# Reading the banks of an attention kernel's filling units behind the next transposes' cast and low part

## The chip, the cores and the metric

One core of a Trainium2 chip runs the whole layer in one launch. The metric is the device time of one execution in microseconds, the median over several runs. A further execution was taken with the hardware profiler; its page and its trace are the source of all shares, waits and rows shown here. The core has a matrix engine (PE, with its weight loads shown as PEld), a vector engine (DVE), a scalar engine (ACT), a general engine (POOL), and SP, whose queue issues the transfers. PE writes to eight banks of PSUM, from which only ACT and DVE read.

## The reference

A decoder layer on 1024 tokens of width 1024: a half feed-forward block, then two kinds of attention side by side, gated and merged, then a second half feed-forward block and a gated embedding. The change lies in the attention stage:

```python
def forgetting_attention(q, k, v, log_f):          # 8 heads of 64; q and k are normalised first
    F = jnp.cumsum(log_f, axis=1)
    logits = q @ k.T * scale + F[t] - F[s]          # causal
    return softmax(logits) @ v

def stick_breaking_attention(q, k, v):             # 8 heads of 64
    z = q @ k.T * scale
    after = reverse_cumsum(log_sigmoid(-z)) - log_sigmoid(-z)
    return exp(log_sigmoid(z) + after) @ v          # strictly causal

merged = (sigmoid(g_fox) * (y_fox @ w_branch_fox)
          + sigmoid(g_sb) * (y_sb @ w_branch_sb))
```

All in float32. The kernel keeps that precision by splitting an operand into a high part, rounded to the matrix engine's float32r format, and a low part, the difference; a product is then three matmuls (high by high, high by low, low by high) or a stacked form of these.

## The kernel before

**Stages.** The first feed-forward block and the norm take about the first 660 us of the profiled execution, the attention loop the time from about 714 to 1376 us, and the branch products, the output product, the second block and the embedding the rest. The feed-forward blocks are written under a manual schedule, where program order is engine order. The attention loop is not: a planner, which has its own estimate of every duration, puts an instruction on its engine's queue when its inputs are ready by that estimate, and takes the one that comes first in program order where several are ready. `order(key, ins)` adds an edge from the last instruction given under the same key, so that instructions under one key ("pe", "act", "dve", "wh", "wl") stand on their queue in program order. All matmuls are under "pe". The queues themselves run in order.

**The loop.** Sixteen heads follow each other, 0 to 7 forgetting ("fox") and 8 to 15 stick-breaking. A head has four steps c = 0 to 3 of two blocks of 128 queries. `scores(step, ...)` makes the two blocks' score products into `sc` banks (L990, L991) and the weights from them: in fox heads a fused add and minimum on DVE (L995), the exponential on ACT (L1001) and a division on POOL (L1003); in stick-breaking heads two sigmoids on ACT (L998, L999), scans on DVE (L966) and products on POOL (L1013, L1017). `apply(prev, ...)` then finishes the step before: for each pair of key blocks, from the last pair down to 0, `transposes(kpair)` puts transposed weights into a `pt` bank (L1042), ACT casts them into a PT buffer (L1044, `high`), DVE subtracts for the low part (L1045, `low`), and `values(kpair + 1)` multiplies the pair before with the values into the `av` bank (L1058). At the end of a step three instructions gather the result from `av` (L1077 to L1079). The values product with both parts in one matmul, and the two additions at L1078 and L1079, stand in the kernel before and after alike.

In stick-breaking heads `high` is under "act" and `low` and the scans under "dve"; the scans of the odd block are held in `later`, and the first part of them is issued behind the first transposes of `apply` (`later.pop(0)()`), the rest behind the last. In fox heads `high` and `low` are under no key.

**Filling units.** Between these pieces PE would wait, so it gets other work: the projections for later heads. A unit is a generator that takes a `pf` bank (there are two), issues 24 matmuls (12 for a branch unit) one at a time, and then reads its bank. Kinds: values (`v_units`, L755, read by L112 and L113), queries and keys of a fox pair, with or without values (`fox_qk_units`, L755, read by L112, L113 and L844 to L846, and after each fourth unit L849 to L852 on DVE and POOL), stacks of a stick-breaking head in two halves (`sb_stack_units`, L763, read in `fill_stacks` by L862 to L865, with the copies L871 and L872 issued on SP), and gates (`g_units`, L763, read by L914 or, from gate 8 on, L916 into a PT buffer, stored by L917 on SP). Weights for the units come by L126 on SP and are split by L136 on ACT and L146 on POOL. PT has three buffers, shared by `high`/`low`, the gates and the squares of the fox units.

`take()` runs the units: the cost of a head's units (0.216 a matmul of 512 columns, 0.109 a smaller one) is divided by 22, and each call issues matmuls until its share is used up. In every head the calls are, for c = 0: one behind each of the two scores, one behind each of four transposes, one ahead of values(0); then 2 + 1 + 1 for c = 1, 2 + 2 + 1 for c = 2, 2 + 3 + 1 for c = 3: 22 in all. At the listed places of `TURNS` the stacks of the next fox head are also made (`fox_stack_units`, L882, which reads its bank on the spot by L867 to L870).

A head's units, as examples: head 8 has the two halves of stick-breaking head 9's stacks and three gate halves; head 10 three value units, two halves of stacks, two gate halves; head 14 one half of stacks, two gate halves, the other half of stacks, a gate half.

Of the kernel before, what the change touches and what calls it, by code (L numbers as in the profile page):

```python
# [11 lines left out]
F32R = mybir.dt.float32r  # L12
# [26 lines left out]
def tile_hybrid_decoder_layer(  # L39
# [56 lines left out]
    def f(ap):  # L96
        return ap.bitcast(F32)
# [667 lines left out]
                yield 0.216  # L765

    loads = []

    def add_load(cell, fn):
        cell["i"] = len(loads)  # L770
# [35 lines left out]
    def v_units(col, extra, cell):  # L806
        n = 256 + extra
        add_load(cell, lambda: mix_nat([(col, col + n)], NAT))

        def unit(t):  # L810
            weights(cell)
            if t == 0:
                cell["v"] = slot("X", [P, NT, 4, P], F32R)
            ps = bank("pf")
            yield from nat_steps(ps, t, cell["w"], n, hT)
            v_out(cell, t, ps[:, :256])
            if extra:
                nc.vector.tensor_copy(lfs[:, t, :], ps[:, 256:264])  # L818
        return [(24 * 0.109, unit(t)) for t in range(NT)]

    def fox_cols(pair):
# [2 lines left out]
    def fox_qk_units(pair, cell, col=None, vcell=None, sq_tag="PT"):  # L824
        cols = fox_cols(pair) + (((col, col + 256),) if col else ())
        nk = 2 if col else 4
        tags = (("WH", "WL"), ("WH", "WL"), ("WH", "WL"), ("Y", "RAW"))
        w = [stage([kp(win)[:, nk * i:nk * i + nk, a:b] for a, b in cols], nk, 1024 // nk, tags[i]) for i in range(KD // nk)]

        def unit(t):  # L830
            if t == 0:
                cell["n"] = [slot("RN", [P, 4, 2, 2, HD]) for _ in range(2)]
                cell["ss"] = [stat([P, 4, 4], "qkss", 4) for _ in range(2)]
            ps = bank("pf")
            yield from nat_steps(ps, t, cell["w"] if "w" in cell else [c["w"] for c in w], 1024 // nk, hT)
            if vcell is not None:
                if t == 0:
                    vcell["v"] = slot("X", [P, NT, 4, P], F32R)
                v_out(vcell, t, ps[:, 256:])
            half, q = divmod(t, 4)  # L840
            N = cell["n"][half]
            src = ps[:, :256].rearrange("p (s h d) -> p s h d", s=2, h=2)
            sq = slot(sq_tag, [P, 256])
            nc.scalar.activation(sq[:].rearrange("p (h s d) -> p s h d", s=2, h=2), src, AF.Square)  # L844
            nc.scalar.copy(N[:, q].rearrange("p h s d -> p s h d"), src)
            nc.vector.reduce_sum(cell["ss"][half][:, q, :], sq[:].rearrange("p (g d) -> p g d", g=4), axis=AX.X)  # L846
            if q == 3:
                ss = cell["ss"][half][:].rearrange("p a b -> p (a b)")
                nc.vector.tensor_scalar(ss, ss, 1.0 / HD, EPS, ALU.mult, ALU.add)  # L849
                nc.gpsimd.tensor_tensor(ss, ss, mhalf[:], ALU.pow)  # L850
                nv = N[:].rearrange("p a h s d -> p (a h s) d")
                nc.gpsimd.tensor_mul(nv, nv, ss.unsqueeze(2).broadcast_to([P, 16, HD]))  # L852
        return [(24 * (0.216 if col else 0.109), unit(t)) for t in range(NT)], w

    def new_stacks():
# [2 lines left out]
    def fill_stacks(stacks, ps, cs, gain=None):  # L858
        Q, KH, KL = stacks
        a, b = slice(0, HD), slice(HD, P)  # L860
        if gain is None:
            nc.scalar.copy(Q[a, cs], ps[a, :])  # L862
            nc.scalar.copy(KH[b, cs], ps[b, :])
            nc.vector.tensor_sub(Q[b, cs], ps[a, :], f(Q[a, cs]))
            nc.vector.tensor_sub(KL[b, cs], ps[b, :], f(KH[b, cs]))  # L865
        else:
            nc.scalar.activation(Q[a, cs], ps[a, :], AF.Copy, scale=gain[a, :])  # L867
            nc.scalar.activation(KH[b, cs], ps[b, :], AF.Copy, scale=gain[b, :])
            nc.vector.scalar_tensor_tensor(Q[b, cs], ps[a, :], gain[a, :], f(Q[a, cs]), ALU.mult, ALU.subtract)
            nc.vector.scalar_tensor_tensor(KL[b, cs], ps[b, :], gain[b, :], f(KH[b, cs]), ALU.mult, ALU.subtract)  # L870
        nc.sync.dma_start(f(KH[a, cs]), f(KH[b, cs]))  # L871
        nc.sync.dma_start(f(KL[a, cs]), f(KL[b, cs]))  # L872
# [14 lines left out]
    def sb_stack_units(head, out_cell):  # L887
        c0 = head * HD

        add_load(out_cell, lambda: wload([kp(win)[:, :, SQ + c0:SQ + c0 + HD], kp(win)[:, :, SK + c0:SK + c0 + HD]], KD, P))  # L890

        def unit(half):
            weights(out_cell)
            if half == 0:
                out_cell["st"] = new_stacks()
            ps = bank("pf")
            yield from feat_steps(ps, half, out_cell["w"])
            fill_stacks(out_cell["st"], ps, slice(half * 512, half * 512 + 512))
        return [(24 * 0.216, unit(0)), (24 * 0.216, unit(1))]

    def g_units(m, tags=None):
        cell = {}
        src = [kp(win)[:, :, GFOX + m * P:GFOX + m * P + P]]
        if tags:
            cell = stage(src, KD, P, tags)
        else:
            add_load(cell, lambda: wload(src, KD, P))

        def unit(half):
            ps = bank("pf")  # L910
            yield from feat_steps(ps, half, cell["w"] if tags else weights(cell))
            g = slot("PT", [P, 512])
            if m < KD:
                nc.vector.tensor_copy(g[:], ps[:])  # L914
            else:
                order("act", nc.scalar.activation(g[:], ps[:], AF.Sigmoid))  # L916
            nc.sync.dma_start(gd[m, :, half * 512:half * 512 + 512], g[:])  # L917
        units = [(24 * 0.216, unit(0)), (24 * 0.216, unit(1))]
        return (units, cell) if tags else units

# [106 lines left out]
    def apply(step, fill, later=()):  # L1027
# [32 lines left out]
        def turn_and_scan(kpair):  # L1060
            transposes(kpair)
            if later and kpair == c:
                later.pop(0)()
            fill()

        turn_and_scan(c)
# [62 lines left out]
    def attention():  # L1129
# [93 lines left out]
        load_fb(0)  # L1223
        ys = {}
        prev = None
        for h in range(16):
            fox = h < 8
            if h % 2 == 0:
                idx = fox_pairs[h // 2] if fox else 4 + (h - 8) // 2
                ys[h // 2] = {"t": slot("Y", [P, S]), "idx": idx}  # L1230
            head = ys[h // 2]["idx"] % 4 * 2 + h % 2
            v = (vf1, vf0, vs0, vs1)[h // 4]
            load_fb(h + 1)
            total = sum(u[0] for u in fill[h])
            state = [0.0 if h else 1.0, 0.0]
            gens = [u[1] for u in fill[h]]

            def take(last=False):
                state[0] += total / 22
                while gens and (last or state[1] < state[0]):  # L1240
                    cost = next(gens[0], None)
                    if cost is None:
                        gens.pop(0)
                    else:
                        state[1] += cost
            for c in range(4):
                y0, y1 = Y_AT.get((h, c), ((), ()))
                split_y(*y0)
                load_y(*y1)
                step = {"fox": fox, "c": c, "head": head, "st": stacks[h], "v": v, "y": ys[h // 2], "last": h == 15}  # L1250
                if fox:
                    step["fb"] = fbs[h]
                later = []
                calls = [0]

                def take_and_turn():
                    take()
                    if (h, c, calls[0]) in TURNS:
                        x, half = TURNS[h, c, calls[0]]
                        run(fst(x, "sc" if calls[0] else "av")[half][1])  # L1260
                    calls[0] += 1
                scores(step, take_and_turn, later if prev is not None else None)
                if prev is not None:
                    apply(prev, take_and_turn, later)
                if (h, c) == (4, 0):
                    place(c2w[3])
                prev = step
            take(True)
        rest = seq(*[g for _, g in fox_branch[8:]])
        apply(prev, lambda: run(islice(rest, 10)))  # L1270
        run(rest)
# [38 lines left out]
    def fox_branch_units():  # L1310
# [4 lines left out]
        def unit(m, half):  # L1315
            if half == 0:
                A.append(slot(("Q", "KH", "KL", "Y", "GF", "RN")[m], [P, S]))
            a = A[m]
            ps = bank("pf")
            yield from branch_steps(ps, 0, m, half, weights(cells[m]))  # L1320
            gated(a[:, half * 512:half * 512 + 512], ps, 0, m, half)
# [398 lines left out]
```

## Time and profile before

| | |
|---|---|
| median of 3 runs | 2234.88 us (2234.82 to 2235.48) |
| profiled execution | 2237.77 us |
| its span, first to last instruction | 2236.1 us |
| PE busy | 2215.4 us (99%) |
| DVE, ACT, POOL busy | 1512.9, 972.0, 812.8 us |
| mean granted TensorE clock | 0.999 |
| attention loop, PE busy in 732 to 1020 us (fox heads) | 277.99 of 288.00 us |
| the same in 1020 to 1376 us (stick-breaking heads) | 353.74 of 356.00 us |

How to read the rows: a line of the timeline has the start in us from the span's start, the duration in us, the engine, the kernel's line (L1045 is line 1045), the operation, output<-inputs, the shape and the count of instructions merged into the line, and in brackets the idle time of the engine just before, with what ended it. PE's ends are modelled and overlap the next start. A line of the waits has the waiting instruction, the one waited for, the total in us, how often, and the longest. A line of the stage table has the stretch, its length, and then the busy time of PE, PEld, DVE, ACT and POOL with their instruction counts, the granted clock, the transfer share and GB/s. "SPq" is SP issuing a transfer.

### The profile page before, as it was taken

The page shows a single profiled execution, that of the slowest core. Times are in us where ns is not written, and L with a number is a line of the kernel's source. Part 1 is how long each engine was busy: PE and PEld are TensorE (multiplying, and loading weights), DVE is VectorE, ACT ScalarE, POOL GpSimd, SP SyncE. Part 2 cuts the span into 40 slices and gives each one's busy share as a digit, 9 for nine tenths or more (in the row PEclk, how much of TensorE's full clock was granted, in tenths as well). Part 3 has the DMA queues.
Part 4 walks back from the last instruction along what each step waited for, and adds up shares of the span by engine and source line. Part 5 has one row for each costly group of instructions (what it writes and reads, how often), then busy time and mean ns, then how long its engine had stood idle before and what let it go on. Part 6 is the DMA issues. An engine that isn't in the chain of part 4 may idle for free.

```text
span 2236.1 us, 28590 instructions
## 1 busy us (share of the span) xinstructions
PE 2215.4 (99%) x10537; PEld 1842.1 (82%) x10537; DVE 1512.9 (68%) x2252; ACT 972.0 (43%) x1694; POOL 812.8 (36%) x709
## 2 busy tenths in 40 slices
PE   9999999999999999999999999999999999999999
PEld 7888888888889888877988888887888888888887
DVE  7855555497885665667667676899755555778873
ACT  6433333333453555455555564255333333433441
POOL 0344444310015456455556654400544443200111
PEclk9999999999999999999999999999999999999999
DMA  8232322484433023132124236741423232655132
GB/s 321 96 121 84 113 99 101 149 296 147 147 126 99 26 86 85 38 104 67 43 71 118 62 122 208 259 144 64 141 88 125 85 127 80 250 202 206 63 117 91
DMA packets 187709, 278.00 MB, mean 124 GB/s; under 512 B 27944, under 2 KB 110120, under 8 KB 187568
## 3 DMA queue, kind: packets, MB, share of 16 engines
q1 hardware_dynamic: 187568, 276.17, 36.8%
q8 instruction: 83, 1.36, 0.3%
q14 instruction: 58, 0.48, 0.1%
HBM read 192.47 MB, written 75.27 MB: 120 GB/s over the span
## 4 chain that ended last, share of the span: by engine, by line
PE 86%; DVE 6%; ACT 3%; issue 2%; DMA 1%; POOL 1%; SPq 0%; ACTq 0%; DVEq 0%; POOLq 0%
PE ps L496 36%; PE ps L388 19%; PE ps L763 8%; PE ps L755 6%; PE ps L1656 4%; PE ps L1301 3%; PE ps L1058 3%; PE ps L1042 2%; PE ps L449 2%; PE ps L991 1%; PE ps L990 1%; PE ps L1351 1%; DVE H L113 1%; DVE RN L966 1%; ACT H L112 1%
## 5 line engine op out<-in xcount | busy, mean ns | idle before, releaser
L388 PE MATMUL ps<-H,H 128*128 128x512 f32 x2184 | 497.3, 389 | 0.0
L388 PEld LDWEIGHTS ps<-H,H 128*128 128x128 f32 x2184 | 409.5, 188 | 84.9
L496 PE MATMUL ps<-H,WL 128*128 128x512 f32 x1008 | 238.9, 389 | 0.0
L496 PEld LDWEIGHTS ps<-H,WL 128*128 128x128 f32 x1008 | 189.2, 188 | 39.3
L763 PE MATMUL ps<-H,WH 128*128 128x512 f32 x640 | 175.9, 401 | 0.0
L1045 DVE TENSOR_TENSOR PT<-ps,PT 128x512 fp32r<-128x512 f32 (+1 forms) x160 | 100.8, 634 | 72.0 <-ACT PT L1044 71.0
L496 PE MATMUL ps<-H,Q 128*128 128x512 f32 x576 | 137.4, 389 | 0.0
L396 DVE SCALAR_TENSOR_TENSOR X<-ps,X 128x512 f32<-128x512 f32 x168 | 108.7, 685 | 41.8 <-PE ps L388 41.7
L763 PEld LDWEIGHTS ps<-H,WH 128*128 128x128 f32 x640 | 113.9, 188 | 19.1
L496 PEld LDWEIGHTS ps<-H,Q 128*128 128x128 f32 x576 | 108.1, 188 | 22.4
L1044 ACT CAST PT<-ps 128x512 fp32r<-128x512 f32 (+1 forms) x160 | 87.0, 548 | 87.3 <-PE ps L1042 82.2
L146 POOL TENSOR_TENSOR WL<-RAW,WH 128x512 fp32r<-128x512 f32 (+1 forms) x92 | 108.9, 1204 | 40.1 <-ACT WH L136 34.6
L496 PE MATMUL ps<-X,WL 128*128 128x512 f32 x480 | 115.5, 389 | 0.0
L209 POOL TENSOR_TENSOR PT<-PT,RN 128x1024 f32<-128x1024 f32 x2 | 4.8, 2402 | 295.1 <-ACT RN L203 295.1
L755 PE MATMUL ps<-WH,H 128*128 128x256 f32 (+2 forms) x576 | 111.2, 323 | 0.2 <-DVE log_f L818 0.2
L1003 POOL TENSOR_TENSOR T<-T,l 128x128 f32<-128x128 f32 (+3 forms) x64 | 73.3, 1147 | 100.1 <-DVE l L1002 99.2
L496 PEld LDWEIGHTS ps<-X,WL 128*128 128x128 f32 x480 | 89.9, 188 | 19.1 <-DVE WL L113 0.5
L496 PE MATMUL ps<-H,PT 128*128 128x512 f32 x432 | 103.2, 390 | 0.2 <-DVE PT L113 0.2
L1058 PE MATMUL ps<-PT,X 128*128 128x512 f32 x320 | 95.6, 380 | 6.8 <-DVE PT L1045 6.6
L283 POOL TENSOR_TENSOR PT<-GF,RN 128x512 f32<-128x512 f32 x20 | 33.1, 1657 | 174.1 <-DVE GF L539 89.8
L496 PEld LDWEIGHTS ps<-H,PT 128*128 128x128 f32 x432 | 80.9, 188 | 18.0 <-DVE PT L113 1.3
L1013 POOL TENSOR_TENSOR T<-T,RN 128x383 f32<-128x383 f32 (+2 forms) x64 | 77.1, 1205 | 46.2 <-DVE RN L966 44.0
(419 smaller groups left out, 4821.2 us busy)
## 6 DMA issues: line engine op xcount, KB each, us to landing
hidden<-PT SPq DMA_DIRECT2D x40, 512.0 KB, 3.1
WH<-in_ffn_w_gate_dram SPq DMA_DIRECT2D x38, 512.0 KB, 5.5
Q<-hidden SPq DMA_DIRECT2D x24, 512.0 KB, 6.6
hidden<-RN SPq DMA_DIRECT2D x22, 512.0 KB, 2.6
KH<-in_ffn_w_up_dram SPq DMA_DIRECT2D x20, 512.0 KB, 6.5
KL<-in_ffn_w_up_dram SPq DMA_DIRECT2D x20, 512.0 KB, 6.9
T<-in_ffn_w_down_dram SPq DMA_DIRECT2D x20, 512.0 KB, 4.5
RAW<-in_w_in_dram SPq DMA_DIRECT2D x18, 512.0 KB, 4.3
```

The costliest lines, as they stand in the source:

```text
L146: ins = eng_lo.tensor_sub(lo[part], raw[part], f(hi[part]))
L388: pe(nc.tensor.matmul(groups[g][t][:], wt[:, b, k, t * P:(t + 1) * P], act[:, a, k, :], start=(fresh and n == 0), stop=(i in (6, 1, 4) and ...
L396: nc.vector.scalar_tensor_tensor(xs, groups[g][t][:], scale, xs, ALU.mult, ALU.add)
L496: pe(nc.tensor.matmul(ps[:], hl[:, a, k, :], rhs(m, b, k), start=(first and i == 0), stop=(final and i == 11), skip_group_check=True))
L755: pe(nc.tensor.matmul(ps[:, :n], hT[t // 4][a][:, k, (t % 4) * P:(t % 4 + 1) * P], w[k // d][b][:, k % d, :n], start=(i == 0), stop=(i == ...
L763: pe(nc.tensor.matmul(ps[:], w[a][:, k, :], hT[half][b][:, k, :], start=(i == 0), stop=(i == 23)))
L1003: nc.gpsimd.tensor_mul(T[:, :n], T[:, :n], l[:].broadcast_to([P, n]))
L1013: nc.gpsimd.tensor_mul(T[:, cut:n - 1], T[:, cut:n - 1], R[:, cut:n - 1])
L1044: high = nc.scalar.copy(pt[:, 0, :width], ps[:, :width])
L1045: low = nc.vector.tensor_sub(pt[:, 1, :width], ps[:, :width], f(pt[:, 0, :width]))
L1058: pe(nc.tensor.matmul(both[:, :, q0:256], v2[:, kb, hd, :], pt[:, :, c0:c0 + 256 - q0], start=(kpair == c and i == 0), stop=(kpair == 0 an ...
L1656: pe(nc.tensor.matmul(ps, pl["w"][d, k // 2][b][:, k % 2, m * P:(m + 1) * P], hT[half][a][:, k, cs], start=(i == 0), stop=(i == 23)))
```

## The change

A unit's reads of its bank become a closure. While the attention loop runs (`put_off[0]` is true) the closure is put on a list `late` instead of being called, and `settle(keep)` calls the oldest ones until `keep` are left. `settle()` stands in `turn_and_scan` behind `transposes` (with its `high` and `low`) and behind the first held scan part, ahead of `fill`; ahead of a `TURNS` entry; and at each head's end. A unit begins with `settle(1)`, where its matmuls have 512 columns, or `settle()`. So the reads come in program order behind the next transposes' `high` and `low`, or at the latest when the unit after next wants the bank. Branch units still read on the spot. In `fill_stacks` without gain (stick-breaking stacks) the two casts are now given to `order` under "act" and the two subtractions under "dve". The diff, cut:

```diff
+    late, put_off = [], [False]
+    def settle(keep=0):
+        while len(late) > keep:
+            late.pop(0)()
+    def finish(fn):
+        if put_off[0]:
+            late.append(fn)
+        else:
+            fn()
...
@@ v_units, unit(t)
+            settle()
             ps = bank("pf")
             yield from nat_steps(ps, t, cell["w"], n, hT)
-            v_out(cell, t, ps[:, :256])
-            if extra:
-                nc.vector.tensor_copy(lfs[:, t, :], ps[:, 256:264])
+            def out():
+                v_out(cell, t, ps[:, :256])
+                if extra:
+                    nc.vector.tensor_copy(lfs[:, t, :], ps[:, 256:264])
+            finish(out)
@@ fox_qk_units, unit(t): settle(1 if col else 0) ahead of the bank; v_out and L839 to L852 become out(), finish(out)
...
@@ fill_stacks
         if gain is None:
-            nc.scalar.copy(Q[a, cs], ps[a, :])
-            nc.scalar.copy(KH[b, cs], ps[b, :])
-            nc.vector.tensor_sub(Q[b, cs], ps[a, :], f(Q[a, cs]))
-            nc.vector.tensor_sub(KL[b, cs], ps[b, :], f(KH[b, cs]))
+            order("act", nc.scalar.copy(Q[a, cs], ps[a, :]))
+            order("act", nc.scalar.copy(KH[b, cs], ps[b, :]))
+            order("dve", nc.vector.tensor_sub(Q[b, cs], ps[a, :], f(Q[a, cs])))
+            order("dve", nc.vector.tensor_sub(KL[b, cs], ps[b, :], f(KH[b, cs])))
@@ sb_stack_units, unit(half)
+            settle(1)
             ps = bank("pf")
             yield from feat_steps(ps, half, out_cell["w"])
-            fill_stacks(out_cell["st"], ps, slice(half * 512, half * 512 + 512))
+            finish(lambda: fill_stacks(out_cell["st"], ps, slice(half * 512, half * 512 + 512)))
@@ g_units, unit(half): settle(1) ahead of the bank; slot, copy or sigmoid and the store become out(), finish(out)
...
@@ apply, turn_and_scan(kpair)
             transposes(kpair)
             if later and kpair == c:
                 later.pop(0)()
+            settle()
             fill()
@@ attention
         prev = None
+        put_off[0] = True
         for h in range(16):
...
                     take()
                     if (h, c, calls[0]) in TURNS:
+                        settle()
...
             take(True)
+            settle()
+        put_off[0] = False
@@ fox_branch_units, unit(m, half)
+            settle(1)
             ps = bank("pf")
```

More of the change, by code (lines that the diff above doesn't have):

```diff
@@ L833, in unit @@
                 cell["ss"] = [stat([P, 4, 4], "qkss", 4) for _ in range(2)]
+            settle(1 if col else 0)
             ps = bank("pf")
             yield from nat_steps(ps, t, cell["w"] if "w" in cell else [c["w"] for c in w], 1024 // nk, hT)
[L836 to L852, printed above, removed]
+            if vcell is not None and t == 0:
+                vcell["v"] = slot("X", [P, NT, 4, P], F32R)
@@ new lines, in out @@
+            def out():
+                if vcell is not None:
+                    v_out(vcell, t, ps[:, 256:])
+                half, q = divmod(t, 4)
+                N = cell["n"][half]
+                src = ps[:, :256].rearrange("p (s h d) -> p s h d", s=2, h=2)
+                sq = slot(sq_tag, [P, 256])
+                nc.scalar.activation(sq[:].rearrange("p (h s d) -> p s h d", s=2, h=2), src, AF.Square)
+                nc.scalar.copy(N[:, q].rearrange("p h s d -> p s h d"), src)
+                nc.vector.reduce_sum(cell["ss"][half][:, q, :], sq[:].rearrange("p (g d) -> p g d", g=4), axis=AX.X)
+                if q == 3:
+                    ss = cell["ss"][half][:].rearrange("p a b -> p (a b)")
+                    nc.vector.tensor_scalar(ss, ss, 1.0 / HD, EPS, ALU.mult, ALU.add)
+                    nc.gpsimd.tensor_tensor(ss, ss, mhalf[:], ALU.pow)
+                    nv = N[:].rearrange("p a h s d -> p (a h s) d")
+                    nc.gpsimd.tensor_mul(nv, nv, ss.unsqueeze(2).broadcast_to([P, 16, HD]))
@@ L853, in fox_qk_units @@
+            finish(out)
         return [(24 * (0.216 if col else 0.109), unit(t)) for t in range(NT)], w
@@ L909, in unit, with out @@
         def unit(half):
+            settle(1)
             ps = bank("pf")
             yield from feat_steps(ps, half, cell["w"] if tags else weights(cell))
[L912 to L917, printed above, removed]
+            def out():
+                g = slot("PT", [P, 512])
+                if m < KD:
+                    nc.vector.tensor_copy(g[:], ps[:])
+                else:
+                    order("act", nc.scalar.activation(g[:], ps[:], AF.Sigmoid))
+                nc.sync.dma_start(gd[m, :, half * 512:half * 512 + 512], g[:])
+            finish(out)
         units = [(24 * 0.216, unit(0)), (24 * 0.216, unit(1))]
@@ L1318, in unit @@
             a = A[m]
+            settle(1)
             ps = bank("pf")
```

## The prediction, made before the changed kernel was run

> **What bounds the kernel now.** I read the page's busy line first, then the stage table of the attention loop (heads 0 to 7 forgetting attention, heads 8 to 15 stick-breaking attention), then who waits for whom on PE in each half, and last the rows around each wait.
>
> ```profile
> span 2236.1 us, 28590 instructions
> PE 2215.4 (99%) x10537; PEld 1842.1 (82%) x10537; DVE 1512.9 (68%) x2252; ACT 972.0 (43%) x1694; POOL 812.8 (36%) x709
> ...
> L388 PE MATMUL ps<-H,H 128*128 128x512 f32 x2184 | 497.3, 389 | 0.0
> ```
> ```profile
> 732.00:1020.00 288.00, 277.99 (x1490) 231.93 (x1489) 179.61 (x560) 155.46 (x331) 157.00 (x160) 0.99 0.24 66
> 1020.00:1376.00 356.00, 353.74 (x1840) 296.64 (x1839) 253.00 (x391) 202.85 (x420) 204.77 (x222) 1.00 0.33 97
> ```
> ```profile
> PE ps L1058 <- DVE PT L1045: 4.8, 8, 1.7
> PE ps L882 <- DVE Y L1079: 3.6, 5, 1.7
> ...
> PE ps L1058 <- DVE PT L1045: 2.2, 8, 0.5
> ```
>
> PE is the bound: 20.7 us of the span are not PE (2236.1 - 2215.4). The stage rows give the loop's part: 288.00 - 277.99 = 10.0 us idle in the fox heads and 356.00 - 353.74 = 2.3 us in the stick-breaking heads. That is all there is to win, plus a little that the profile hides: the modelled end of a matmul (389 ns) lies behind the point where the next one could start (497.3 / 2184 = 0.228 us), so a shown idle of 0.17 us is a lateness of up to 0.17 + 0.389 - 0.228 = 0.33 us. The waits (first two lines: fox heads; third: stick-breaking heads) say that the values (L1058) wait for the low part (L1045) for 4.8 and 2.2 us, and the turned stacks (L882) for the last addition out of the av bank (L1079).
>
> **The change part by part.** No instruction is added or removed, so PE's work stays. What moves is the reading of the `pf` bank of a filling unit: the ACT copies or sigmoid, the DVE parts, POOL's power and product after every fourth query/key unit (L850, L852), and the issues on SP (gate stores L917, stack copies L871 and L872). They are now issued behind the next `high` and `low` (and behind the first scan part, which `later.pop(0)` issues before `settle`). For the stack halves four `order` calls are new: they stand in the same fixed chains on ACT and DVE as the stick-breaking heads' casts, lows and scans.
>
> *Where it helps.* Heads 8, 11, 12 and 13 hand out 25.9 (5 units x 24 x 0.216) in 22 takes (calls of the filler), 1.18 each; the second stack half ends at 10.4 / 1.18, in take 9, which is that of the second scores of step 1. Head 8 there:
>
> ```profile
> 1045.37 0.58 ACT L862 CAST Q<-ps 64x512 fp32r<-64x512 f32 x1
> 1045.43 0.49 PE L1042 MATMUL ps<-identf,T 128*128 128x128 f32 x3
> ...
> 1046.57 0.48 ACT L1044 CAST PT<-ps 128x384 fp32r<-128x384 f32 x1
> 1046.57 0.69 DVE L864 TENSOR_TENSOR Q<-ps,Q 64x512 fp32r<-64x512 f32 x1 [1.69 <-ACT KH L863]
> ...
> 1047.27 0.69 DVE L865 TENSOR_TENSOR KL<-ps,KH 64x512 fp32r<-64x512 f32 x1
> ...
> 1048.00 0.56 DVE L1045 TENSOR_TENSOR PT<-ps,PT 128x384 fp32r<-128x384 f32 x1
> ...
> 1048.61 0.62 PE L1058 MATMUL ps<-PT,X 128*128 128x512 f32 x2 [0.17 <-DVE PT L1045]
> ```
> ```profile
> 1176.08 0.62 PE L1058 MATMUL ps<-PT,X 128*128 128x512 f32 x2 [0.17 <-DVE PT L1045]
> ```
> ```profile
> 1216.53 0.61 PE L1058 MATMUL ps<-PT,X 128*128 128x512 f32 x2 [0.16 <-DVE PT L1045]
> ```
> ```profile
> 1257.86 0.62 PE L1058 MATMUL ps<-PT,X 128*128 128x512 f32 x2 [0.16 <-DVE PT L1045]
> ```
>
> The transposes are there at 1045.92, but L862, L863, L864 and L865 go first; the low part ends at 1048.56 and the values are late. With the change the cast can start at 1045.95 and the low part ends near 1047.1 (0.48 + 0.56 later, and a handover), over a microsecond before the values: all four waits go. Price: between the shown 0.17 and the 0.33 worked out above; I take 0.33, because matmul steps, not modelled ends, set the next start. Gain 4 x 0.33 = **1.3 us**. Behind the low part nothing of this step waits for the two subtractions; the copies of the stack (L871, L872) are wanted by the next head only.
>
> *Where it costs.* Where the half settles at a call of `turn_and_scan` that also issues scans and is followed by another low part in the same step, the chain is low, scans, two subtractions, low. By the count of takes this is so three times: head 10 (28.6 / 22 = 1.30 a take, three value units of 2.6 first) ends its halves in takes 11 and 15, so they settle at transposes 1 of step 2 and transposes 2 of step 3; head 14's last half ends in take 18 and settles at transposes 2 of step 3.
>
> ```profile
> 1139.52 0.56 DVE L1045 TENSOR_TENSOR PT<-ps,PT 128x384 fp32r<-128x384 f32 x1 [1.53 <-ACT PT L1044]
> ...
> 1140.44 1.59 DVE L966 TENSOR_TENSOR_SCAN RN<-GF,RN 128x255 f32<-128x255 f32 x1
> ...
> 1141.96 0.66 DVE L1045 TENSOR_TENSOR PT<-ps,PT 128x512 fp32r<-128x512 f32 x1
> 1142.65 0.68 DVE L864 TENSOR_TENSOR Q<-ps,Q 64x512 fp32r<-64x512 f32 x1
> ...
> 1143.28 0.62 PE L1058 MATMUL ps<-PT,X 128*128 128x512 f32 x2
> ...
> 1143.35 0.70 DVE L865 TENSOR_TENSOR KL<-ps,KH 64x512 fp32r<-64x512 f32 x1
> ```
> ```profile
> 1150.95 1.87 DVE L966 TENSOR_TENSOR_SCAN RN<-GF,RN 128x383 f32<-128x383 f32 x1
> 1152.74 1.30 DVE L1045 TENSOR_TENSOR PT<-ps,PT 128x512 fp32r<-128x512 f32 x2
> ```
> ```profile
> 1153.92 0.62 PE L1058 MATMUL ps<-PT,X 128*128 128x512 f32 x2
> ```
> ```profile
> 1313.23 0.68 DVE L864 TENSOR_TENSOR Q<-ps,Q 64x512 fp32r<-64x512 f32 x1 [0.30 <-ACT KH L863]
> ...
> 1314.65 0.56 DVE L1045 TENSOR_TENSOR PT<-ps,PT 128x384 fp32r<-128x384 f32 x1
> ...
> 1317.21 1.26 DVE L1045 TENSOR_TENSOR PT<-ps,PT 128x512 fp32r<-128x512 f32 x2
> ...
> 1317.92 0.73 PE L1058 MATMUL ps<-PT,X 128*128 128x512 f32 x2 [0.43 <-DVE PT L1045]
> ```
>
> First place: the scans end at 1142.03; 0.68 + 0.70 = 1.38 of subtractions put the next low part to 1143.4 to 1144.1, and the values that start at 1143.28 today come at 1144.15: +0.85. Second: scans end at 1152.82, the subtractions at 1154.2, the low part at 1154.85; values today at 1153.92: +0.9. Third: today the subtractions stand ahead of the first low part; behind the change low, scans and subtractions follow from about 1313.75 (the cast's end) as 0.56 + 2.1 + 1.38, so the next low part ends near 1318.45 where today it ends near 1317.85: +0.6. Sum **+2.35 us**. Bounds: 0 each if the scans come so late that the planner's slack swallows them, 1.38 each (4.1) if nothing does.
>
> *Fox heads: 0.* Their casts, lows and evictions have no fixed chain; a planner places each when its inputs are ready, and program order only breaks ties. The trace shows it: an instruction of later scores runs between the two additions of an earlier step.
>
> ```profile
> 899.68 0.40 DVE L995 CUSTOM_DVE_ANT_0 T<-GF,ps,m 128x192 f32<-128x192 f32 x1
> ...
> 900.01 0.41 DVE L1079 TENSOR_TENSOR Y<-ps,Y 64x256 f32<-64x256 f32 x1
> ```
>
> So most evictions stay where they are; the waits on L1079 (3.6 us) have L995 and the additions themselves in front, not units. Units before a `TURNS` entry are settled there, at the place where they are issued today, L850 and L852 with them. The largest wait of the loop is a queue matter:
>
> ```profile
> 865.71 1.39 SPq L126 DMA_DIRECT2D RAW<-in_w_in_dram  x3
> 867.15 0.47 SPq L917 DMA_DIRECT2D gates<-PT  x1
> ...
> 870.77 0.59 ACT L1044 CAST PT<-ps 128x512 fp32r<-128x512 f32 x1 [2.23 <-DMA gates<-PT]
> ...
> 872.13 0.73 PE L1058 MATMUL ps<-PT,X 128*128 128x512 f32 x2 [1.67 <-DVE PT L1045]
> ```
> ```profile
> 874.00:875.00 1.00, 1.00 (x3) 0.73 (x3) 0.82 (x5) 0.49 (x2) 1.00 (x2) 0.50 0.00 0
> ```
>
> A gate store stands on SP behind three weight loads, and the cast waits for the PT slot that the store holds. The change issues this store even later relative to the loads (the next unit's `fetch` now comes first), so I leave the wait in: 0. Bounds: gone, with the half clock that follows it (0.50 in the row; the clock was below one from 873 to 877, about 1.7 us lost), is -3.4; a second one like it is +3.4. A rule bears on the new 0.9 us waits: the Trainium skill, TensorE: Matmul & The Clock Gate, HAM oscillation, says that only PE gaps of more than about 3.4 us drop the clock. By it they cost no clock and the sum stands. The row shows a drop behind an idle of 1.67 us, which differs, and another of the loop's waits could cost the same, so I hold 1.7 us for the upper end.
>
> **Sum.** -1.3 + 2.35 + 0 = about **+1.0 us**. The profiled execution took 2237.77 us (span 2236.1) and would take 2238.8; the runs' median is 2234.88, so I forecast **2235.9 us**. A change below 0.2% (4.5 us) is about what a measurement of this kernel cannot tell from none.
>
> **Rivals.**
> 1. *The waits simply go.* The order chain costs nothing (scans late enough, DVE free) and the later PT slot ends the 1.67 us wait: -1.3 - 3.4 = -4.7, **2230.2 us**, just faster. For it: four identical waits with the evictions in front. Against: the SP order above.
> 2. *The chain bites everywhere* (the slower side). Place: DVE in heads 8 to 14, two subtractions of 1.38 us between a scan and the next low part; at 0.85 each it decides from seven of the 14 halves issued there: 7 x 0.85 - 1.3 = +4.7; eight give **2240.4 us**. For it: DVE is 71% busy there (253.00 / 356). Against: the count of takes puts eleven of the halves where no low part follows a scan in the same step.
> 3. *Held banks.* Two `pf` banks; if the unit after next finds its bank unread, PE waits through the copy and the subtractions, 0.58 + 0.68 + 0.70 = 1.96 us; it decides from three. At each of seven head starts: 7 x 1.96 - 1.3 = +12.4, **2247.3 us**. Against: the longest run of takes without transposes is three (last fill, two scores), and a unit of 24 matmuls needs more than four at 5 to 6 matmuls each, so two units cannot end unread. The Trainium skill, PSUM — Partial Sum Buffer, Summary: rules for kernel authors, says "Evacuate promptly"; by it this rival is the case, and today's rows, where units are read on the spot, cannot show it.
> 4. *It does nothing that shows.* The planner puts nearly all back: **2234.9 us**. For it: the L995 row; against: the new fixed chain in heads 8 to 14.
>
> **How the numbers follow.** Forecast (-0.5 to +3 us) 0.50; rival 4 0.18, both within 0.2%; rival 1 0.14, nearly all faster; rival 2 0.12 and rival 3 0.06, slower. So faster 0.13, same 0.69, slower 0.18. Low end 2230.0: rival 1. High end 2240.5: forecast plus the uncapped subtractions (1.8) plus a lost clock (1.7), or rival 2 at eight. This leaves out rival 3 and the tails of 1 and 2.
>
> **What would show it.** Right: the waits at the four rows (step 1 of heads 8, 11, 12, 13) gone, cast before L862; in head 10, steps 2 and 3, L864 and L865 between a scan and L1045, and L1058 waiting 0.6 to 0.9 us twice; PE idle of the stick-breaking half near 2.3 us still; the fox half near 10 us. Wrong: a fox half several microseconds off 10 (evictions did matter there, or the SP order changed), a changed wait of L1044 for a gate store, PE waiting at a unit's first matmul (L763, L755) for a read of `pf`, or another stretch at half clock.

## The result, and the profile after

The changed kernel is slower: 2249.60 us (median of four runs, 2248.09 to 2250.99) against 2235.18 us (four runs, 2234.82 to 2235.48), a ratio of 1.0064 with the 95% interval [1.0047, 1.0082]. That is 14.4 us more, 13.7 us above the forecast and 9 us above the upper end of its range. Medians here and below are of all runs, ratios and intervals of the fast runs alone (three of the experiments hold one slow run each, of 3157 to 3624 us), and a ratio need not be the quotient of its medians.

The page of the changed kernel, its busy line; then the two stage rows of the attention loop (stretch, length, busy PE, PEld, DVE, ACT and POOL with counts, granted clock, transfer share, GB/s). In the changed kernel the stick-breaking heads end near 1385 us where they ended at 1376.

```profile
span 2246.2 us, 28571 instructions
PE 2217.7 (99%) x10537; PEld 1844.1 (82%) x10537; DVE 1521.2 (68%) x2252; ACT 971.4 (43%) x1694; POOL 812.9 (36%) x709
```
```profile
732.00:1020.00 288.00, 278.81 (x1493) 231.04 (x1492) 182.68 (x559) 155.11 (x332) 158.31 (x161) 1.00 0.24 66
1020.00:1385.00 365.00, 353.79 (x1828) 297.96 (x1828) 256.66 (x388) 201.55 (x417) 202.95 (x220) 0.99 0.32 94
```

The fox heads idle 9.2 us (10.0 before). The stick-breaking heads idle 365.00 - 353.79 = 11.2 us, where 2.3 were idle before. Who waits on PE, first over the whole span, then in the stick-breaking half alone:

```profile
PE ps L763 <- DVE KL L884: 9.0, 2, 5.8
PE ps L1082 <- DVE PT L1069: 7.4, 12, 2.0
PE ps L901 <- DVE Y L1104: 1.8, 5, 0.5
```
```profile
PE ps L1082 <- DVE PT L1069: 1.9, 3, 1.0
```

The first line is new: twice, a unit's first matmul (L763) waits for the second subtraction of a stack half (L884, L865 before), 9.0 us in all. Both places lie in head 10. PE's rows there, from the end of the first stack half on:

```profile
1130.67 1.52 PE L763 MATMUL ps<-H,WH 128*128 128x512 f32 x6
...
1132.96 1.55 PE L763 MATMUL ps<-H,WH 128*128 128x512 f32 x6
...
1135.05 1.09 PE L763 MATMUL ps<-H,WH 128*128 128x512 f32 x4
1135.98 0.63 PE L763 MATMUL ps<-H,WL 128*128 128x512 f32 x2
1136.44 0.49 PE L1066 MATMUL ps<-identf,T 128*128 128x128 f32 x3
1136.69 1.64 PE L763 MATMUL ps<-H,WL 128*128 128x512 f32 x6
1138.16 0.60 PE L1066 MATMUL ps<-identf,T 128*128 128x128 f32 x4
1142.00 2.66 PE L763 MATMUL ps<-H,WH 128*128 128x512 f32 x6 [3.24 <-DVE KL L884]
...
1151.68 0.49 PE L1066 MATMUL ps<-identf,T 128*128 128x128 f32 x3
1157.95 2.90 PE L763 MATMUL ps<-H,WH 128*128 128x512 f32 x6 [5.77 <-DVE KL L884]
```

The first half is complete by about 1130.67, when the second half takes the other `pf` bank. That one fills in exactly four takes of six matmuls (1130.67, 1132.96, 1135.05 to 1135.98, 1136.69), and the next unit, of gate 8, wants the first half's bank at 1142.00 - 3.24 = 1138.76. The first transposes behind the first half, and so the first place where its reads may be issued, stand at 1136.44, one take ahead of that. At the second place there is not even one: the transposes at 1151.68 are followed at once by the unit of gate 9, which wants the second half's bank (1157.95 - 5.77 = 1152.18). DVE's rows at both places, at the second with the cast on ACT:

```profile
1137.92 0.56 DVE L1069 TENSOR_TENSOR PT<-ps,PT 128x384 fp32r<-128x384 f32 x1 [1.76 <-ACT PT L1068]
...
1138.85 1.57 DVE L990 TENSOR_TENSOR_SCAN RN<-GF,RN 128x255 f32<-128x255 f32 x1
1140.44 0.68 DVE L883 TENSOR_TENSOR Q<-ps,Q 64x512 fp32r<-64x512 f32 x1
1141.16 0.69 DVE L884 TENSOR_TENSOR KL<-ps,KH 64x512 fp32r<-64x512 f32 x1
```
```profile
1152.71 0.55 ACT L1068 CAST PT<-ps 128x384 fp32r<-128x384 f32 x1
...
1153.29 0.56 DVE L1069 TENSOR_TENSOR PT<-ps,PT 128x384 fp32r<-128x384 f32 x1 [1.07 <-ACT PT L1068]
1153.77 0.74 DVE L990 TENSOR_TENSOR_SCAN RN<-GF,mask_sb 128x128 f32<-128x128 f32 x1
1154.55 1.83 DVE L990 TENSOR_TENSOR_SCAN RN<-GF,RN 128x383 f32<-128x383 f32 x1
1156.41 0.69 DVE L883 TENSOR_TENSOR Q<-ps,Q 64x512 fp32r<-64x512 f32 x1
1157.11 0.69 DVE L884 TENSOR_TENSOR KL<-ps,KH 64x512 fp32r<-64x512 f32 x1
```

Read the first block from its end: the subtraction that frees the bank ends at 1141.85, because it stands behind a scan of 1.57 us, which stands behind a low part that waited for the cast. In the second block the cast itself starts only at 1152.71, half a microsecond after the bank is wanted. The view of that line alone says how far the read moved (groups of L864 before and of L883 after: two instructions in head 10, with the starts of the first and last):

```profile
L864 DVE TENSOR_TENSOR Q<-ps,Q x2: 683/684/684, 1133.8 to 1142.7; 64x512 fp32r<-64x512 f32 x2
```
```profile
L883 DVE TENSOR_TENSOR Q<-ps,Q x2: 683/684/685, 1140.4 to 1156.4; 64x512 fp32r<-64x512 f32 x2
```

6.6 us later for the first half and 13.7 us for the second. Behind each wait PE also runs at half its clock (stage rows around the two places):

```profile
1142.00:1145.70 3.70, 3.70 (x10) 2.96 (x11) 1.50 (x2) 0.00 (x0) 1.43 (x2) 0.54 0.84 177
...
1155.90:1162.80 6.90, 4.85 (x14) 3.92 (x15) 2.30 (x4) 1.06 (x2) 3.06 (x3) 0.51 0.46 114
```

That costs 3.70 x 0.46 + 4.85 x 0.49 = 4.1 us of matmul time. The two profiled executions then add up: PE's idle grew from 20.7 to 2246.2 - 2217.7 = 28.5 us, +7.8; PE's busy time grew by 2.3 us (the 4.1 here less the 1.7 that the kernel before lost at 873 to 877); together 10.1, the difference of the spans. The medians differ by 14.4 because the profiled execution of before (2237.77 us) lies 2.6 above its median and that of after (2248.09 us) 1.5 below.

### The profile page after: what moved, and what is told of

It is laid out like the page before. It is cut to its first block, busy times and chain, and to the rows that moved or that the text cites. A ratio compares the mean times of both kernels' runs of the same rounds, so it can differ in the third digit from the quotient of the medians.

```text
span 2246.2 us, 28571 instructions
## 1 busy us (share of the span) xinstructions
PE 2217.7 (99%) x10537; PEld 1844.1 (82%) x10537; DVE 1521.2 (68%) x2252; ACT 971.4 (43%) x1694; POOL 812.9 (36%) x709
## 4 chain that ended last, share of the span: by engine, by line
PE 85%; DVE 7%; ACT 3%; issue 2%; DMA 1%; POOL 1%; SPq 0%; ACTq 0%; POOLq 0%; DVEq 0%
PE ps L496 35%; PE ps L388 18%; PE ps L763 9%; PE ps L755 6%; PE ps L1686 4%; PE ps L1330 3%; PE ps L1082 3%; PE ps L1066 2%; PE ps L449 2%; PE ps L1015 1%; DVE RN L990 1%; PE ps L1014 1%; PE ps L1381 1%; DVE H L113 1%; DVE T L1019 1%
## 5 line engine op out<-in xcount | busy, mean ns | idle before, releaser
L763 PE MATMUL ps<-H,WH 128*128 128x512 f32 x640 | 179.1, 407 | 9.0 <-DVE KL L884 9.0
L763 PEld LDWEIGHTS ps<-H,WH 128*128 128x128 f32 x640 | 116.2, 192 | 29.2 <-issue 9.4
L146 POOL TENSOR_TENSOR WL<-RAW,WH 128x512 fp32r<-128x512 f32 (+1 forms) x92 | 108.6, 1201 | 40.7 <-ACT WH L136 35.0
L990 DVE TENSOR_TENSOR_SCAN RN<-GF,RN 128x127 f32<-128x127 f32 (+2 forms) x96 | 97.8, 1019 | 2.6
```

The lines of the kernel that those rows point to most:

```text
L146: ins = eng_lo.tensor_sub(lo[part], raw[part], f(hi[part]))
L763: pe(nc.tensor.matmul(ps[:], w[a][:, k, :], hT[half][b][:, k, :], start=(i == 0), stop=(i == 23)))
L990: order("dve", nc.vector.tensor_tensor_scan(*args))
```

## Experiments

A first group asks whether the fixed chain in head 10 holds the banks, or the deferral by itself.

**The chain left out.** The changed kernel without the four `order` calls:

```diff
-            order("act", nc.scalar.copy(Q[a, cs], ps[a, :]))
+            nc.scalar.copy(Q[a, cs], ps[a, :])
...
-            order("dve", nc.vector.tensor_sub(KL[b, cs], ps[b, :], f(KH[b, cs])))
+            nc.vector.tensor_sub(KL[b, cs], ps[b, :], f(KH[b, cs]))
```

> The changed kernel with the four order calls in fill_stacks taken out again, so the reads are put off but the planner places the stack's subtractions freely. Theory A (the loss is PE waiting at a unit's first matmul for a pf bank whose subtractions the chain holds behind two scans, twice in head 10, 9.0 us idle, and the half clock behind it): both waits of L763 on L884 go, PE idle of the loop falls by about 9 us, time 2233 to 2237. Rival B (putting the reads off holds banks too long, chain or not): waits on L884 stay, time 2243 or more.

Measured: 2236.07 us against 2235.58, ratio 1.0003 [0.9994, 1.0012]. No unit waits for L884. The view of L883 in head 10 and the start of head 11:

```profile
L883 DVE TENSOR_TENSOR Q<-ps,Q x3: 683/684/685, 1133.6 to 1165.0; 64x512 fp32r<-64x512 f32 x3
```

The first read stands at 1133.6 again, as in the kernel before (1133.8), the second at 1143.7 (1142.7 before); the third is that of head 11. Issued later in program order but under no key, it is put by the planner where its input is ready. So the deferral alone holds no bank; it needs the chain.

**Head 10 read on the spot,** all other heads put off (`put_off[0] = h != 10` at the head of the loop):

> The changed kernel with the reads put off in all heads but head 10, where they are issued at the unit's end; the chain stays. Theory A: the two waits go, the four removed waits of the values in heads 8, 11, 12 and 13 stay removed, time 2232.5 to 2236. Rival C (the loss is spread: the chain delays DVE in all heads 8 to 14): at most a fourth of the 14 us comes back, time 2244 or more. Rival D (the loss is in the fox heads or the clock alone): time stays near 2249.

Measured: 2236.66 us against 2235.58, ratio 1.0005 [0.9996, 1.0014], just above what was expected; the two waits on L884 are gone. The whole loss hangs on head 10, and what the other heads gain does not show in the time.

**The chain alone:** the kernel before with the four `order` calls, and nothing put off.

> The kernel before with only the four order calls added; reads stay at the unit's end. Theory A: the chain alone holds no bank, since the subtractions are issued ahead of the next scans: time within 1.5 us of before, 2234 to 2237, no wait of L763 on a subtraction. Rival C: the chain itself costs, 2240 or more.

Measured: 2235.05 us against 2235.58, ratio 0.9996 [0.9987, 1.0005]. A chain whose reads are issued on the spot costs nothing that shows. Chain and deferral are each harmless; together they hold the bank.

**The reads ahead of the scan:**

```diff
             transposes(kpair)
+            settle()
             if later and kpair == c:
                 later.pop(0)()
-            settle()
             fill()
```

> The changed kernel with settle ahead of the held scan part instead of behind it: the subtractions stand directly behind the low part. Theory A: both waits of head 10 stay but lose the scans' time, about 1.9 us each: from 3.2 to about 1.5 us and from 5.8 to about 3.6 us, for the copies and the subtractions still come behind the next cast; time 2242 to 2247. Rival E (the scans alone are the cause): both waits vanish, time 2233 to 2236.

Measured: 2243.25 us against 2235.58, ratio 1.0036 [1.0024, 1.0049]. PE's two rows:

```profile
1141.59 1.63 PE L763 MATMUL ps<-H,WH 128*128 128x512 f32 x6 [1.77 <-DVE KL L884]
...
1153.89 2.90 PE L763 MATMUL ps<-H,WH 128*128 128x512 f32 x6 [3.69 <-DVE KL L884]
```

The waits shrink from 3.24 and 5.77 to 1.77 and 3.69 us. The scans were 3.5 of the 9.0 us of waiting; the other 5.5 come from reads that the chain puts behind the transposes' cast and low part, whatever follows these.

The second group asks what is left of the change without the held bank.

**Another bank for the waiting unit,** with DVE's order in head 10 as in the change:

```diff
-            ps = bank("pf")
+            ps = bank("sc" if (m, half) == (8, 1) else "pf")
```

> The changed kernel with one bank changed: the gate unit behind head 10's second stack half (gate 8, second half) takes an sc bank instead of a pf bank; all queues keep their order. Theory A (PE waits for the bank, not for the late subtractions as such): both waits of L763 on L884 go, since the next pf user comes a unit later; what stays are the two waits of the values that the prediction priced, 0.85 and 0.9 us, at steps 2 and 3 of head 10; time 2235.5 to 2239. Rival G (the order of the queues itself costs, whoever waits): PE loses the same 9 us at another place, time 2245 or more.

Measured: 2238.16 us against 2234.94, ratio 1.0013 [1.0004, 1.0022]. The chain is unchanged, its victim is another:

```profile
1143.79 0.69 DVE L883 TENSOR_TENSOR Q<-ps,Q 64x512 fp32r<-64x512 f32 x1
1144.51 0.69 DVE L884 TENSOR_TENSOR KL<-ps,KH 64x512 fp32r<-64x512 f32 x1
1145.23 0.69 DVE L1069 TENSOR_TENSOR PT<-ps,PT 128x512 fp32r<-128x512 f32 x1
```
```profile
1145.98 0.72 PE L1082 MATMUL ps<-PT,X 128*128 128x512 f32 x2 [0.79 <-DVE PT L1069]
...
1158.01 0.72 PE L1082 MATMUL ps<-PT,X 128*128 128x512 f32 x2 [0.79 <-DVE PT L1069]
```

With the bank out of the way, the values wait for the low part behind the subtractions, twice 0.79 us shown. This is what the prediction priced at 0.85 and 0.9.

**Head 10 alone put off** (`put_off[0] = h == 10`):

> The changed kernel with the reads put off in head 10 alone (all other heads at the unit's end; the chain stays). Theory A: this alone brings the whole loss, two waits of L763 on L884 of about 3.2 and 5.8 us and the half clock behind them, 2247 to 2251. Rival C (loss spread over heads 8 to 14): a fourth of it at most, 2240 or less.

Measured: 2248.50 us against 2234.94, ratio 1.0059 [1.0047, 1.0072]. One head brings the whole loss. Its profiled execution (2250.77 us) has the same waits and a longer first stretch at half clock:

```profile
PE ps L763 <- DVE KL L884: 8.7, 2, 5.5
```
```profile
1141.00:1148.00 7.00, 6.03 (x15) 4.81 (x16) 2.41 (x4) 0.00 (x0) 2.39 (x3) 0.51 0.43 94
1158.20:1165.00 6.80, 6.16 (x17) 4.92 (x18) 1.19 (x2) 1.08 (x2) 1.64 (x3) 0.50 0.53 138
```

**The four heads with a gain** (`put_off[0] = h in (8, 11, 12, 13)`):

> The changed kernel with the reads put off in heads 8, 11, 12 and 13 alone, where the four waits of the values stood. Theory A: those four waits go and nothing is added but the small waits seen behind them: 0.5 to 1.3 us below before, 2233.5 to 2235. Rival H (a removed wait comes back at a later values product of the same head): no difference from before, or up to 1 us above it.

Measured: 2234.97 us against 2234.94, ratio 0.9998 [0.9989, 1.0007]. The waits of the stick-breaking half on the low part:

```profile
PE ps L1082 <- DVE PT L1069: 1.2, 3, 0.6
```

They were 2.2 us in eight before. The four waits of 0.16 and 0.17 us that the prediction named are gone, 0.66 us together. The rest of the fall is mixed: a wait of 0.30 us at 1162.95 is gone too, but it is also gone with the chain alone; the 0.47 us at 1236.26 is gone, but 0.58 us is new one step later, at the first values product of head 13 (1241.48), and 0.15 us in head 8 (1055.96). So theory A is right about the four waits, and rival H's pattern, a removed wait that comes back at a later values product, is seen too, though in the next head. The time does not move.

**Fox heads alone** (`put_off[0] = h < 8`):

> The changed kernel with the reads put off in the fox heads (0 to 7) alone. Theory A: the planner puts them by readiness, so time moves by less than 1.5 us either way: 2234 to 2237. Rival D (the fox heads have a share in the loss): 2239 or more.

Measured: 2237.91 us against 2234.94, ratio 1.0009 [1.0000, 1.0018], above what was expected. PE idles no more in these heads than before (288.00 - 278.43 = 9.6 us against 10.0), so waiting does not show the 2 us. The wait that stood at 872.13 with 1.67 us is longer:

```profile
874.67 0.73 PE L1082 MATMUL ps<-PT,X 128*128 128x512 f32 x2 [2.07 <-DVE PT L1069]
```

The last group takes the prediction's own sum apart, and tries for a kernel that beats both.

**Stick-breaking heads alone, with the other bank** (`put_off[0] = h >= 8`, and the bank as above):

> The change in heads 8 to 15 only (fox heads read on the spot), and with the unit of gate 8's second half in an sc bank, so that no unit waits for a held pf bank. This is the prediction's own sum without its two errors. Theory A (the prediction's terms were right apart from the hold and the fox heads): -1.3 + 0.85 + 0.9 + 0.6 = +1.05 us on the kernel before, 2235.0 to 2237.0 where before is about 2235; waits of the values on the low part near 1146 and 1158 us of about 0.8 us each, none on KL in front of a unit. Theory B (the stick-breaking heads cost more than the sum says, and the fox heads nothing): 2237.5 to 2239, as with all heads put off.

Measured: 2236.47 us against 2235.46, ratio 1.0004 [0.9996, 1.0013]. The two waits of head 10 are there:

```profile
1142.69 0.73 PE L1082 MATMUL ps<-PT,X 128*128 128x512 f32 x2 [0.79 <-DVE PT L1069]
1154.44 0.73 PE L1082 MATMUL ps<-PT,X 128*128 128x512 f32 x2 [0.78 <-DVE PT L1069]
```

+1.0 us between the medians, where the sum said +1.05; the interval reaches from -0.9 to +2.9 us, so it fits the sum without proving its size. The trace says the same: the values' waits of the stick-breaking half come to 3.4 us in this run, 2.2 before.

**The same with the reads ahead of the scan:**

> The change in heads 8 to 15 only, with the other bank as in the run before, and with the reads issued ahead of the first held scan part instead of behind it: the two subtractions stand behind the low part, the scans behind them. Meant to beat both kernels. Theory A: the subtractions end 2 to 2.6 us earlier, but the second low part still stands behind scans and subtractions together, 2 x 0.69 us later than with reads on the spot, so the two waits of about 0.8 us in head 10 stay and the time is within 1 us of the run before it, 2234.5 to 2237. Theory B: what hurts is the scan ahead of the subtractions alone; then these waits go, and the four waits of heads 8, 11, 12, 13 stay gone: 2232.5 to 2234.5, under the kernel before.

Measured: 2235.72 us against 2235.46, ratio 1.0004 [0.9995, 1.0012]; the two waits are 0.99 and 0.95 us. It does not beat the kernel before: whether the subtractions stand ahead of the scan or behind it, the next low part stands behind both.

**Fox heads alone, gates read on the spot** (in `g_units`, `out()` in place of `finish(out)`):

> The change in fox heads only, with the gates read on the spot (values, queries and keys still put off). It asks where the roughly 2 us of the fox heads come from. Theory A (the gate store is issued later on SP, behind the weight loads, holds its PT slot longer and delays a cast): the wait of the values near 872 us is back to 1.7 us or less and the time at 2234.5 to 2236.5. Theory B (the moved reads of values, queries and keys on ACT, DVE and POOL cost it, as the new waits of 0.4 and 0.6 us near 841 and 861 us in the fox-only run): those waits stay and the time is 2237 to 2238.5.

Measured: 2237.11 us against 2235.46, ratio 1.0001 [0.9992, 1.0010]. The wait of the values is 1.85 us at 874.17, so theory A's wait did not come back to 1.7. Of theory B's two waits the one near 861 stays (0.59 us at 861.05), the one near 841 is gone, and the median lies in its range, at the lower end. But the interval of the ratio holds no difference at all, so neither theory is shown, and the 2 us of the fox heads stay without a cause.

## Why the prediction was wrong

**The step that failed** is the count in rival 3, "two units cannot end unread", and with it the chance of 0.06 and its use of takes as the measure. In head 10 it is true that no two units ended unread. But the count asks when a read is issued, and PE waits for when it has run. It was also too generous: it said that a unit needs more than four takes, and here one filled in exactly four takes of six matmuls. From the settling call to the wanted bank there was one take in step 2 of head 10 and none in step 3, 2.3 and 0.5 us of PE work from the start of the transposes (1136.44 to 1138.76, 1151.68 to 1152.18); the queue from there to the end of L884 took 5.4 and 6.1 us (to 1141.85 and 1157.80). The prediction had the chain, low, scans, two subtractions, at exactly these two places, and asked only who waits for the next low part. The unit that wants the bank comes first on PE, so it pays. The prediction did name this among its signs of being wrong: PE waiting at a unit's first matmul for a read of `pf`, and another stretch at half clock.

**The size in rival 3 was too small as well.** Its price of 1.96 us is a copy and two subtractions with nothing ahead of them; measured are 3.24 and 5.77 us. Two places sufficed where it "decides from three". And it left out the clock: 4.1 us. That its 2247.3 us comes near the measured 2249.6 is luck: it added up seven waits at head starts, where the runs show two longer ones inside head 10. The range has a slip of its own: forecast, 1.8 and 1.7 add up to 2239.4, so only the eight places of rival 2 (2240.4) reach the upper end of 2240.5.

**The terms, one by one.** By the waits and the clock of the profiled execution, the difference of 13.7 us to the forecast is 9.0 of waits and 4.1 of clock, less the 1.75 of late low parts that the longer waits cover: 11.4. The rest, some 2 us, has the size of the fox-only run's loss, or of the longer stretch at half clock in other executions (below); which of the two was not shown.

- *Four waits gone, -1.3 us*: the four went, 0.66 us of shown wait; the rest of the 1.3, which the prediction took to be hidden in the modelled ends, no run shows. Of the three waits left in the stick-breaking half of the changed kernel, the first, in head 8, is new, and so is the second, at the first values product of head 13, which did not wait before, while the 0.47 us at 1236.26 is gone:

```profile
1056.21 0.73 PE L1082 MATMUL ps<-PT,X 128*128 128x512 f32 x2 [0.17 <-DVE PT L1069]
...
1255.11 0.62 PE L1082 MATMUL ps<-PT,X 128*128 128x512 f32 x2 [0.74 <-DVE PT L1069]
...
1328.05 0.73 PE L1082 MATMUL ps<-PT,X 128*128 128x512 f32 x2 [1.04 <-DVE PT L1069]
```

- *Late low parts of head 10, +0.85 and +0.9*: place and size right, but visible only with the bank out of the way: 0.79 and 0.79 us of shown wait, each with up to 0.16 us hidden in the modelled ends (0.389 - 0.228).
- *Head 14, +0.6*: right in place and size. The wait of 0.43 us at 1317.92 is 1.04 in the last of these rows, +0.6. But it does not need the chain, as the prediction had it: without the chain it is 1.05 us (1316.11 in that run), and there too the subtractions run ahead of the next low part.
- *Fox heads, 0*: right for the waiting, open for the time. PE idles 9.2 us there in the changed kernel and 9.6 in the fox-only run, against 10.0, and the planner does put back what is under no key (the chainless run shows it in head 10). Yet the fox-only run is 2.0 us slower in ratio, [0.0, 4.0]. The waits on the additions read 1.8 us against 3.6, but that fall is not shown to come from the change: other runs with the fox heads put off have 2.0 to 3.1 us, runs with these heads as before 2.9 to 4.1.
- *The wait behind the gate store stays*: right, 1.96 us at 873.99 in the changed kernel, 2.07 in the fox-only run.
- *Clock*: the prediction held 1.7 us for one more stretch; the two stretches behind the held banks cost 4.1.

The Trainium skill, PSUM — Partial Sum Buffer, Summary: rules for kernel authors, speaks against a late read with its "Evacuate promptly", which the prediction cited and set aside; here it was right, by 9.0 us of waiting in the changed kernel. The page gives the small size of PSUM as its reason and no time.

## What to carry to other kernels

When a read of an accumulator bank is moved behind other work, write down two times for every bank: when the next user wants it, and when the read will have *run* on its in-order queue, with everything queued ahead of it. Counting in program order how many units are outstanding does not replace this. A tie of a deferred instruction to a fixed chain should be tried apart from the deferral: here each alone cost nothing that showed, and both together cost 14 us.

## What the runs showed of the hardware

How long PE idles does not by itself say whether the clock drops. Shown idles of 1.67 us (before, 872.13), 1.88 us (another bank, 874.49) and 2.07 us (fox-only run) were followed by about 3.4 us at half clock, idles of 1.96 us (changed kernel) and 1.98 us (chain left out) at the same place by none. The kernel before has both cases in one execution: its other idle of 1.67 us was followed by none. The rows of that idle and of the stretch behind it, then the stretches behind the idles in the fox-only run and in the changed kernel:

```profile
900.57 0.63 PE L882 MATMUL ps<-identf,RN 128*128 128x128 f32 x4 [1.67 <-DVE Y L1079]
```
```profile
901.00:904.00 3.00, 3.00 (x18) 2.60 (x17) 2.16 (x8) 2.59 (x5) 1.25 (x1) 1.00 0.00 0
```
```profile
876.30:879.70 3.40, 3.40 (x11) 2.72 (x10) 1.85 (x9) 0.92 (x4) 3.40 (x3) 0.51 0.32 104
```
```profile
874.00:880.00 6.00, 6.00 (x30) 4.96 (x31) 3.15 (x12) 3.05 (x8) 5.77 (x6) 1.00 0.31 94
```

The same 3.24 us of idle in front of the first unit was followed by about 3.4 us at half clock in one execution (2248.09 us) and went with about 7 in another, the first of them within the idle itself (2250.77 us, head 10 alone). The four runs of the changed kernel stand in two pairs, 2248.09 and 2248.49, 2250.71 and 2250.99; that the length of this stretch parts them fits, and was not shown. The Trainium skill, TensorE: Matmul & The Clock Gate, HAM oscillation, warns of gaps over about 3.4 us; the idles of 1.67, 1.88, 2.07 and 3.24 us were shorter and were followed by half clock all the same, so the measurement decides: a shown idle of 1.67 us can be enough. What else decides was not shown.

A scan's time is no fixed price either. The scan in front of the first held read (128x255) took 1.57 us, beside a weight split on POOL (L146, 1138.47 to 1141.47). In the run with the reads ahead of the scan it took 0.75 us (1142.34), after that split had ended (1142.02). That POOL is the cause was not shown: another scan of this shape beside L146 in the changed kernel (1083.93) took 0.73 us.
